# First adaLN part of a diffusion layer: eight channel tiles taken as four pairs, three of them in column blocks, with the context projections summed pair by pair

## Chip, cores and metric

The kernel runs on one core of a Trainium2 chip. The metric is the device time of one execution in microseconds (us). A difference of less than 0.2% (about 2.2 us) cannot be told from no change.

## What is computed

One layer over 1024 latent tokens and 256 context tokens, 1024 channels each. Cut to what the change touches:

```python
sh1, sc1, ... = split(silu(c) @ w_ada + b_ada, 6)            # latents
csh1, csc1, ... = split(silu(c_ctx) @ w_ada + b_ada, 6)      # context
h_l = LN0(x)   * (1 + sc1)  + sh1     # 1024 tokens
h_c = LN0(ctx) * (1 + csc1) + csh1    # 256 tokens
p = h @ W_in                          # context needs only its k, v and gate columns
```

The rest of the layer (gMLP gating, mLSTM, output projection, MLP) follows and is the same in both kernels.

## The kernel before

The first part of the program, about 112 us, makes the shifts and scales `mod1`, the normalized context and its k, v and gate projections, and then the v and gate projection of the eight latent chunks of 128 tokens. After it come the q and k projections of the latents (`qk`).

The reduction over 1024 channels is cut into eight tiles of 128 (`KT` = 8). `ada1_load(j)` (L119) loads, for output channel tile j, the shift and scale columns of `w_ada` for all eight reduction tiles: two loads of 512 KB. `ada1_mm(j)` (L273) multiplies them by the two conditioning vectors, which stand as 2 of 128 columns of a weight tile: five reduction tiles in float32, which TensorE runs as two passes each, and three split into a high and a low part, three products each (`mm3`). The operands are 256 columns wide. `ada1_fin` (L288) transposes the 2x256 result and adds the bias into `mod1`. The eight tiles follow each other on TensorE, and work of the next tile stands between the parts of the last.

Context: `norm_x` normalizes both context tiles on VectorE, with the power on GpSimd; their transposes stand in PSUM until `ctx_affine(j)` (L305) applies `mod1` for each tile, and `ctx_split` (L311) makes the pair `Hhi`, `Hlo` of four tiles at a time. Then come the k projection (`kctx`) and `vg_chunk` (L356) for the two context tiles, each a sum over eight reduction tiles into one PSUM bank, emptied by ScalarE (`kcr`, `va`).

Latents: `lat_h(c)` (L395) normalizes chunk c, transposes it on TensorE (`pt_l`), applies `mod1` in eight ScalarE instructions (`h_l`), casts them to `Hhi` and leaves the rest in `Hlo` on VectorE; `vg_chunk(c)` is then 48 matmuls of 264 columns. A scheduler settles the order on each engine from dependencies and its own estimates; all loads are issued from one queue (SP), in order, and a load waits there for the buffer that it fills.

Of the kernel before, what the change touches and what calls it, by code (L numbers as in the profile page):

```python
# [38 lines left out]
def layer_kernel(ctx: ExitStack, tc: tile.TileContext, I: dict, out: bass.AP, dbg=None):  # L39
    nc = tc.nc  # L40
    V, S, G, T = nc.vector, nc.scalar, nc.gpsimd, nc.tensor

# [45 lines left out]
    def prep_slot(src, n, name, colscale=None):  # L88
        hi = wpool.tile([P, SLOT], F32R, tag="whi", name=f"hi_{name}")
        lo = wpool.tile([P, SLOT], F32R, tag="wlo", name=f"lo_{name}")  # L90
        h = n // 2
        for i in range(2):
            raw = raw_tile(f"raw_{name}_{i}")
            dma(raw[:, :h], src[:, i * h : (i + 1) * h])
            if colscale is not None:
                rv = raw[:, :h].rearrange("p (k c) -> p k c", k=2)
                V.tensor_tensor(rv, rv, colscale.unsqueeze(1).broadcast_to([P, 2, h // 2]), ALU.mult)
            S.copy(hi[:, i * h : (i + 1) * h], raw[:, :h])
            V.tensor_tensor(
                lo[:, i * h : (i + 1) * h], raw[:, :h], hi[:, i * h : (i + 1) * h].bitcast(F32), ALU.subtract  # L100
            )
        return hi, lo
# [8 lines left out]
    def x_tile(name):  # L111
        return sp.tile([P, D], F32, tag="x", bufs=7, name=name)
# [6 lines left out]
    def ada1_load(j):  # L119
        rw = [x_tile(f"wa{j}_{i}") for i in range(2)]  # L120
        for i in range(2):
            dma(rw[i], I["wada1"][j, :, i * D : (i + 1) * D])
        hi = wpool.tile([P, SLOT], F32R, tag="whi", name=f"ahi_{j}").rearrange("p (k c) -> p k c", c=264)
        lo = wpool.tile([P, SLOT], F32R, tag="wlo", name=f"alo_{j}").rearrange("p (k c) -> p k c", c=264)
        rv = [t.rearrange("p (k c) -> p k c", c=256) for t in rw]
        for i in range(2):
            k0 = max(KT - ADA_SPLIT, 4 * i)
            if k0 < 4 * i + 4:
                src, ks = rv[i][:, k0 - 4 * i :, :], slice(k0, 4 * i + 4)
                S.copy(hi[:, ks, 0:256], src)  # L130
                V.tensor_tensor(lo[:, ks, 0:256], src, hi[:, ks, 0:256].bitcast(F32), ALU.subtract)
        ada_w.append((hi, lo, rv))
# [164 lines left out]
    xc = []
    for c in range(NCTX):
        ada1_load(2 + c)
        xc.append(load_x(I["ctx"][c * P : (c + 1) * P, :], f"c{c}"))  # L300
    zc = [norm_x(xc[c], f"c{c}") for c in range(NCTX)]
    zt = None
    hc = [sp.tile([P, KT, P], F32, tag="h32", bufs=2, name=f"hc{c}") for c in range(NCTX)]

    def ctx_affine(j):  # L305
        for c in range(NCTX):
            S.activation(
                hc[c][:, j, :], zt[c][j // 4][:, j % 4, :], AF.Identity, bias=mod1[:, j, 0, 1:2], scale=mod1[:, j, 1, 1:2]
            )

    def ctx_split(k0):  # L311
        for c in range(NCTX):
            sl = slice((ctx_tok + c) * P, (ctx_tok + c + 1) * P)
            S.copy(Hhi[:, k0 : k0 + 4, sl], hc[c][:, k0 : k0 + 4, :])
            V.tensor_tensor(
                Hlo[:, k0 : k0 + 4, sl], hc[c][:, k0 : k0 + 4, :], Hhi[:, k0 : k0 + 4, sl].bitcast(F32), ALU.subtract
            )

    prev = None
    for j in range(KT):  # L320
        if 4 <= j + 3 < KT:
            ada1_load(j + 3)
        if j == 4:
            wK = prep_slot(I["win"][0], 2048, "K")
        ar = ada1_mm(j)
        if j == 3:
            zt = [
                h_transpose(zc[0], [ps_tr("zc0a"), ps_tr("zc0b")]),
                h_transpose(zc[1], [ps_mm(f"zc1{q}").rearrange("p (k t) -> p k t", k=4) for q in range(2)]),
            ]  # L330
        if prev is not None:
            ada1_fin(*prev)
            if prev[0] == 3:
                for q in range(4):
                    ctx_affine(q)
                ctx_split(0)
            if prev[0] > 3:
                ctx_affine(prev[0])
        prev = (j, ar)
# [40 lines left out]


    for b in range(2):
        pm = ps_mm(f"kctx_{b}")
# [4 lines left out]
        S.copy(raw[:, 1:257], pm[:, :256])  # L388
# [3 lines left out]

    xs = [load_x(I["x"][c * P : (c + 1) * P, :], f"l{c}") for c in range(2)]

    def lat_h(c):  # L395
        if c + 2 < NT:
            xs.append(load_x(I["x"][(c + 2) * P : (c + 3) * P, :], f"l{c + 2}"))
        z = norm_x(xs[c], f"l{c}")
        h_tile(sp, z, c, lambda kt: mod1[:, kt, 1, 0:1], lambda kt: mod1[:, kt, 0, 0:1], f"l{c}", 2)

    vg_chunk(ctx_tok, NT)
    lat_h(0)
    vg_chunk(ctx_tok + 1, NT + 1)
    lat_h(1)
# [1277 lines left out]
```

## Time and profile before

| | us |
|---|---|
| median of 3 runs | 1098.2 (1096.82 to 1098.74) |
| the profiled execution | 1095.39 |
| its span, first to last instruction | 1093.4 |
| around the span | 2.0 |
| TensorE busy | 1061.6 (97%) |
| VectorE, ScalarE, GpSimd busy | 744.1, 542.2, 54.9 |

The profiled execution is 2.8 us below the median. Times in the trace count from the start of the span. The mean granted TensorE clock over the span is 0.996 of full speed.

### The profile page before, as it was taken

To read this page: it belongs to the slowest core of one execution; us is meant where nothing else is said; L and a number is where in the kernel's file an instruction comes from. 1 tells how busy PE (TensorE), PEld (TensorE's weight loads), DVE (VectorE), ACT (ScalarE), POOL (GpSimd) and SP (SyncE) were. 2 spreads that over 40 slices of the span, in tenths; PEclk is the share of its full clock that TensorE was granted. 3 is DMA by queue.
4 is the path that set the end of the run, shared out by engine and by line. 5 is a ranking of instruction groups with operands and counts; after the bars stand their busy time and mean duration, and the time that the engine had idled before them with its cause. 6 is when DMAs were issued, how large, how long until landed. Compare 5 with 4: busy or idle time off the path is not lost.

```text
span 1093.4 us, 14625 instructions
## 1 busy us (share of the span) xinstructions
PE 1061.6 (97%) x5279; PEld 882.6 (81%) x5279; DVE 744.1 (68%) x1294; ACT 542.2 (50%) x909; POOL 54.9 (5%) x81
## 2 busy tenths in 40 slices
PE   8999999998989999999999999999999999999996
PEld 6899778777878888878888888888888888888885
DVE  5793576587773477689946556475577556868966
ACT  3576453344451255677756556566444233435511
POOL 0010000001110021100000000000000000001201
PEclk9999999999999999999999999999999999999998
DMA  9783478878683953342726252537996328655501
GB/s 331 253 293 103 125 253 294 265 195 222 150 229 122 315 175 117 106 165 68 269 89 206 93 186 112 173 135 263 361 388 228 116 97 278 207 189 160 207 1 77
DMA packets 92416, 208.09 MB, mean 190 GB/s; under 512 B 10036, under 2 KB 31412, under 8 KB 92088
## 3 DMA queue, kind: packets, MB, share of 16 engines
q1 hardware_dynamic: 92344, 207.16, 57.4%
q8 instruction: 41, 0.67, 0.2%
q14 instruction: 31, 0.25, 0.1%
HBM read 155.91 MB, written 51.21 MB: 189 GB/s over the span
## 4 chain that ended last, share of the span: by engine, by line
PE 84%; DMA 6%; DVE 5%; ACT 3%; POOL 1%; issue 1%; SPq 0%; DVEq 0%; POOLq 0%; ACTq 0%
PE A L1025 30%; PE B L1025 24%; PE wo L218 3%; PE wo L216 3%; PE wo L217 3%; PE pa L279 2%; DMA nmb<-d_rows 2%; PE vg L218 2%; PE vg L217 2%; PE vg L216 2%; PE u L216 1%; DMA ad<-in_wada 1%; PE u L217 1%; PE u L218 1%; DMA raw_V<-in_win 1%; PE n L748 1%
## 5 line engine op out<-in xcount | busy, mean ns | idle before, releaser
L1025 PE MATMUL A<-wh,pb 128*128 128x512 f32 (+1 forms) x528 | 158.9, 383 | 0.0
L1025 PE MATMUL B<-wh,pb 128*128 128x512 f32 x384 | 118.6, 390 | 0.0
L1025 PEld LDWEIGHTS A<-wh,pb 128*128 128x128 f32 x528 | 98.0, 188 | 20.0
L1025 PE MATMUL A<-wl,pb 128*128 128x512 f32 (+1 forms) x264 | 101.4, 384 | 0.4 <-DVE pm L1552 0.4
L1025 PEld LDWEIGHTS B<-wh,pb 128*128 128x128 f32 x384 | 72.1, 188 | 15.6
L1025 PE MATMUL B<-wl,pb 128*128 128x512 f32 x192 | 75.0, 391 | 0.0
L916 POOL TENSOR_TENSOR rs_n<-ve_n,mhalf 128x1 f32<-128x1 f32 x23 | 29.8, 1294 | 708.8 <-DVE ve_n L914 670.2
L1152 DVE TENSOR_TENSOR wc<-w1x,wc 128x512 fp32r<-128x512 f32 x56 | 38.5, 690 | 35.6 <-ACT wc L1151 35.6
L1245 ACT CAST wh<-b 128x1024 fp32r<-128x1024 f32 x40 | 41.8, 1049 | 41.7 <-DVE pb L1246 29.1
L1245 ACT CAST pb<-a_S 128x1024 fp32r<-128x1024 f32 x32 | 33.7, 1052 | 57.9 <-PE B L1025 24.4
L1246 DVE TENSOR_TENSOR wl<-b,wh 128x1024 fp32r<-128x1024 f32 x40 | 48.7, 1222 | 19.3 <-ACT wh L1245 10.2
L1025 PEld LDWEIGHTS A<-wl,pb 128*128 128x128 f32 x264 | 49.6, 188 | 10.9 <-ACT wh L1245 0.8
L216 PE MATMUL wo<-lo_W,yh 128*128 128x512 f32 x128 | 52.1, 407 | 0.0
L1245 ACT CAST pb<-a_A 128x1024 fp32r<-128x1024 f32 x24 | 25.2, 1052 | 54.0 <-PE A L1025 37.4
L218 PE MATMUL wo<-hi_W,yl 128*128 128x512 f32 x128 | 50.6, 395 | 0.0
L217 PE MATMUL wo<-hi_W,yh 128*128 128x512 f32 x128 | 50.5, 394 | 0.0
L1246 DVE TENSOR_TENSOR pb<-a_S,pb 128x1024 fp32r<-128x1024 f32 x32 | 39.1, 1222 | 12.6 <-ACT pb L1245 12.4
L216 PE MATMUL vg<-lo_VG,Hhi 128*128 128x264 f32 x160 | 46.0, 288 | 0.0
L1246 DVE TENSOR_TENSOR pb<-a_A,pb 128x1024 fp32r<-128x1024 f32 x24 | 29.3, 1222 | 24.3 <-ACT pb L1245 24.3
L1151 ACT CAST wc<-w1x 128x512 fp32r<-128x512 f32 x56 | 34.6, 619 | 22.7 <-PE A L1025 11.0
L218 PE MATMUL vg<-hi_VG,Hlo 128*128 128x264 f32 x160 | 45.3, 284 | 0.6 <-DVE Hlo L207 0.6
L217 PE MATMUL vg<-hi_VG,Hhi 128*128 128x264 f32 x160 | 45.4, 284 | 0.0
(417 smaller groups left out, 2705.0 us busy)
## 6 DMA issues: line engine op xcount, KB each, us to landing
ad<-in_wada SPq DMA_DIRECT2D x32, 512.0 KB, 5.4
b<-in_w SPq DMA_DIRECT2D x32, 512.0 KB, 5.0
a_S<-d_S SPq DMA_DIRECT2D x32, 512.0 KB, 4.2
d_S<-hF SPq DMA_DIRECT2D x50, 256.0 KB, 2.3
a_A<-d_A SPq DMA_DIRECT2D x24, 512.0 KB, 5.0
d_A<-hF SPq DMA_DIRECT2D x36, 256.0 KB, 2.1
wa<-in_wada SPq DMA_DIRECT2D x16, 512.0 KB, 7.1
w1y<-in_w SPq DMA_DIRECT2D x16, 512.0 KB, 4.0
```

The costliest lines, as they stand in the source:

```text
L216: T.matmul(o, ahi, blo, start=start, stop=False)
L217: T.matmul(o, ahi, bhi, start=False, stop=False)
L218: T.matmul(o, alo, bhi, start=False, stop=stop)
L279: T.matmul(pa[:, 0:256], s32[:, k, :], rv[k // 4][:, k % 4, :], start=(k == 0), stop=(k == KT - 1))
L748: T.matmul(pn[d][:, hh, :], nmb[:, d, h, :], vc[:, h, :], start=hh == 0, stop=False, skip_group_check=True)
L916: G.tensor_tensor(rs, ve, mhalf[:, :1], op=ALU.pow)
L1025: T.matmul(o, a, b, start=start and i == 0, stop=stop and i == 2, skip_group_check=more)
L1151: S.copy(t[:, 0:512], src)
L1152: V.tensor_tensor(t[:, 512:1024], src, t[:, 0:512].bitcast(F32), ALU.subtract)
L1245: S.copy(hi, src)
L1246: V.tensor_tensor(lo, src, hi.bitcast(F32), ALU.subtract)
```

## The change

The eight channel tiles become four pairs, with 512 columns (two tiles, shift and scale) in each matmul, all in float32. Pair 0 uses the whole array. Pairs 1 to 3 use 32 of its columns for each matmul: reduction tile k stands in column block k mod 4, so four partial sums stand in four blocks of 32 PSUM partitions, and a matmul by `quads` (a 0/1 matrix) adds and transposes them in `ada1_fin`. The split of `w_ada` on ScalarE and VectorE goes away. The context is normalized on ScalarE; transposes, affine step and split go pair by pair (`ctx_tr`, `ctx_h`), and the k, v and gate sums of the context are held open in five PSUM banks and added to as a pair comes (`ctx_k`, `ctx_vg`). The order on TensorE, VectorE and ScalarE is pinned to the order of the code up to the second latent chunk's `Hlo` (`in_order`); what follows on VectorE and ScalarE is queued after it (`queue_after`). The loads of w_ada are four times two of 1 MB.

```diff
-    def ada1_load(j):
...
+    def ada1_load(p):
+        ws = [wpool.tile([P, SLOT], F32, tag=("whi", "wlo")[i], name=f"wa_{p}_{i}") for i in range(2)]
+        for i in range(2):
+            dma(ws[i][:, :2048], I["wada1"][2 * p + i])
+        ada_w.append([w[:, :2048].rearrange("p (k c) -> p k c", c=512) for w in ws])
...
+    def norm_x(xt, name, on_act=False, mvrs=None):
+        mv, rs = mvrs or stats(sp, xt, D, name)
...
+        if on_act:
+            nb = sp.tile([P, 1], F32, tag="nb", name=f"nb_{name}")
+            V.scalar_tensor_tensor(nb, mv[:, 0:1], -1.0, rs, ALU.mult, ALU.mult)
+            S.activation(z, xt, AF.Identity, bias=nb, scale=rs)
...
+    def ada1_mm(p):
+        pa = bank(7, f"pa_{p}")
+        wide = p < ADA_WIDE
         for k in range(KT):
+            rhs = ada_w[p][k // 4][:, k % 4, :]
+            if wide:
+                T.matmul(pa, s32[:, k, :], rhs, start=k == 0, stop=k == KT - 1)
             else:
+                o = 32 * (k % 4)
+                T.matmul(
+                    pa[o : o + 32, :],
+                    s32[:, k, 0:32],
+                    rhs,
+                    start=k < 4,
+                    stop=k >= 4,
+                    tile_position=(0, o),
+                    skip_group_check=True,
                 )
+        n = 2 if wide else P
+        ar = sp.tile([P, 512], F32, tag="arow", name=f"arow_{p}")
+        V.tensor_copy(ar[:n], pa[:n])
         return ar
...
+    pins = ExitStack()
+    pins.enter_context(in_order(T, V, S))
+    ar = ada1_mm(0)
+    zc = [norm_x(xc[c], f"c{c}", True) for c in range(NCTX)]
+    pt = ctx_tr(0)
+    ada1_fin(0, ar)
+    ctx_h(0, pt)
+    pt = ctx_tr(1)
+    ar = ada1_mm(1)
+    wK, wVG = slot_tiles("K"), [slot_tiles("VG0")]
+    slot_half(wK, rawK[0], 2048, 0)
+    ada1_fin(1, ar)
+    slot_half(wK, rawK[1], 2048, 1)
+    rawVG.append(raw_load(I["wvg"][1], 2112, "VG1"))
+    ada1_load(3)
+    xs = [load_x(I["x"][c * P : (c + 1) * P, :], f"l{c}") for c in range(2)]
+    ctx_h(1, pt)
...
+    ctx_k(0)
+    pt = ctx_tr(2)
+    ctx_k(1)
+    ctx_vg(0, 0)
+    ctx_vg(1, 0)
+    ar = ada1_mm(2)
+    ada1_fin(2, ar)
+    ctx_h(2, pt)
+    pt = ctx_tr(3)
...
+    ctx_k(2)
+    ctx_vg(2, 0)
+    ar = ada1_mm(3)
+    ada1_fin(3, ar)
+    mv0 = stats(sp, xs[0], D, "l0")
+    ctx_h(3, pt)
+    for p in range(3):
+        ctx_vg(p, 1)
...
+    zl = [norm_x(xs[0], "l0", False, mv0), norm_x(xs[1], "l1")]
+    lat_h(0, zl[0])
+    ctx_k(3)
+    for i in range(2):
+        ctx_vg(3, i)
...
+    lat_h(1, zl[1])
+    pins.close()
+    queue_after(pins, V, S)
     wQ = prep_slot(I["win"][1], 2048, "Q")
```

Three places show how the built programs stand. The first is TensorE around the normalized context. `pa` is an adaLN sum, `z_c0` and `z_c1` are the two normalized context tiles, `ptc_` their transposes for a pair, `pat` the transposed sum. Before, at the fourth of eight channel tiles:

```order
L279 MATMUL pa_3_330<-wa3_0_211,s32_186 128x256 x4
L279 MATMUL pa_3_330<-wa3_1_212,s32_186 128x256
L197 MATMUL zc0a_347<-cst_95,z_c0_230 128x128 x4
L197 MATMUL zc0b_348<-cst_95,z_c0_230 128x128 x4
L291 MATMUL pat_2_367<-cst_95,arow_2_315 128x2 x2
```

Now, between pair 0 and pair 1:

```order
L307 MATMUL pa_0_209<-wa_0_1_88,s32_181 128x512 x4
L348 MATMUL ptc_0_246<-cst_91,z_c0_229 128x128
L348 MATMUL ptc_0_246<-cst_91,z_c1_242 128x128
...
L328 MATMUL pat_0_251<-cst_91,arow_0_218 128x2 x4
L348 MATMUL ptc_1_263<-cst_91,z_c0_229 128x128
L348 MATMUL ptc_1_263<-cst_91,z_c1_242 128x128
...
L310 MATMUL pa_1_268<-wa_1_0_188,s32_181 32x512 x4
L310 MATMUL pa_1_268<-wa_1_1_189,s32_181 32x512 x4
```

Eight of the sixteen context transposes now stand between the first and the second quarter of the adaLN matmuls; before, the first stood behind half of them.

The second is ScalarE from the cast of latent chunk 0 to the affine step of chunk 1. Before:

```order
L367 COPY va_9_704<-vg_9_0_706 128x2x128
L206 CAST Hhi_107<-h32_l0_693 128x8x128
L367 COPY va_9_704<-vg_9_1_734 128x2x128
L98 CAST hi_Q_797<-raw_Q_0_799 128x1024
L204 ACTIVATE h32_l1_786<-pt_l1_0_776,mod1_109 128x128 x4
```

Now:

```order
L234 CAST Hhi_104<-h32_l0_529 128x8x128
L488 COPY kcr0_576<-kctx_204 128x256
L467 ACTIVATE kct_0_580<-kcr0_576,convw_317 128x256
L470 ACTIVATE kct_0_580<-kct_0_580 128x256
L488 COPY kcr1_586<-kctx_204 128x256
L467 ACTIVATE kct_1_590<-kcr1_586,convw_317 128x256
L470 ACTIVATE kct_1_590<-kct_1_590 128x256
L443 COPY va_8_596<-vgc_0_0_205 128x2x128
L443 COPY va_8_596<-vgc_0_1_207 128x2x128
L443 COPY va_9_605<-vgc_1_0_206 128x2x128
L443 COPY va_9_605<-vgc_1_1_208 128x2x128
L232 ACTIVATE h32_l1_626<-pt_l1_0_616,mod1_106 128x128 x4
```

All ten instructions that empty the context sums (four of them the convolution of k, `kct`) now stand between the two latent chunks. Before, the convolution stood ahead of both chunks, and two `va` copies and one half of the cast of the q weights stood between them.

The third is TensorE at the transposes of latent chunks 2 and 3. Before:

```order
L218 MATMUL vg_0_1_837<-hi_VG1_527,Hlo_108 128x264
L197 MATMUL pt_l2_0_879<-cst_95,z_l2_877 128x128 x4
L197 MATMUL pt_l2_1_880<-cst_95,z_l2_877 128x128 x4
L216 MATMUL vg_1_0_902<-lo_VG0_518,Hhi_107 128x264
```

Now:

```order
L246 MATMUL vg_1_1_770<-hi_VG1_406,Hlo_105 128x264
L225 MATMUL pt_l2_0_719<-cst_91,z_l2_717 128x128 x4
L225 MATMUL pt_l2_1_720<-cst_91,z_l2_717 128x128 x4
L225 MATMUL pt_l3_0_812<-cst_91,z_l3_810 128x128 x4
L225 MATMUL pt_l3_1_813<-cst_91,z_l3_810 128x128 x4
L244 MATMUL vg_2_0_835<-lo_VG0_282,Hhi_104 128x264
```

Before, the transposes of chunk 2 stood one whole chunk of matmuls (`vg_1`) ahead of the matmuls that use them; now they stand behind `vg_1`, and the matmuls of chunk 2 follow at once.

## Rows read from the trace of the kernel before

**Rows 1.** The page: busy time, share of the span and instructions of each engine.

```profile
PE 1061.6 (97%) x5279; PEld 882.6 (81%) x5279; DVE 744.1 (68%) x1294; ACT 542.2 (50%) x909; POOL 54.9 (5%) x81
```

**Rows 2.** Waits of TensorE: total us, times, longest us.

```profile
PE pa L279 <- DMA wa<-in_wada: 4.9, 1, 4.9
PE kctx L216 <- DVE Hlo L315: 1.6, 1, 1.6
```

**Rows 3.** Timeline of TensorE, adaLN and context k: start, us, what.

```profile
4.93 4.40 PE L279 MATMUL pa<-wa,s 128*128 128x256 f32 x10 [4.93 <-DMA wa<-in_wada]
10.23 2.32 PE L279 MATMUL pa<-wa,s 128*128 128x256 f32 x10
...
37.82 0.28 PE L291 MATMUL pat<-cst,arow 2*128 2x2 f32 x2
...
43.38 0.28 PE L217 MATMUL kctx<-Hhi,hi_K 128*128 128x256 f32 x1
43.50 0.28 PE L218 MATMUL kctx<-Hhi,lo_K 128*128 128x256 f32 x1
```

**Rows 4.** Timeline of TensorE, latent chunks to the first qk matmul.

```profile
59.49 0.37 PE L216 MATMUL vg<-lo_VG,Hhi 128*128 128x264 f32 x1
...
61.00 0.39 PE L218 MATMUL vg<-hi_VG,Hlo 128*128 128x264 f32 x1 [0.56 <-DVE Hlo L207]
...
66.42 1.04 PE L197 MATMUL pt_l<-cst,z_l 128*128 128x128 f32 x8
...
73.10 1.04 PE L197 MATMUL pt_l<-cst,z_l 128*128 128x128 f32 x8
...
112.32 0.48 PE L216 MATMUL qk<-Hlo,hi_K 128*128 128x512 f32 x1
```

**Rows 5.** Windows: stretch, length, busy time of engines, granted clock, DMA share, GB/s.

```profile
5.00:15.00 10.00, 10.00 (x46) 8.48 (x47) 3.18 (x7) 2.50 (x3) 0.00 (x0) 1.00 1.01 371
```

**Rows 6.** Timeline of VectorE, single instructions.

```profile
10.43 0.41 DVE L285 COPY arow<-pa 2x256 f32<-2x256 f32 x1 [2.46 <-PE pa L218]
...
20.50 1.28 DVE L187 BATCH_NORM_STATS2 st_c<-x_c 128x6 f32<-128x512 f32 x2
...
23.52 0.81 DVE L259 TENSOR_SCALAR z_c<-x_c,mv_c,rs_c 128x1024 f32<-128x1024 f32 x1 [0.54 <-POOL rs_c L180]
...
38.40 1.20 DVE L99 TENSOR_TENSOR lo_K<-raw_K,hi_K 128x1024 fp32r<-128x1024 f32 x1
...
46.81 0.48 DVE L377 SCALAR_TENSOR_TENSOR kct<-kcr,convw,kct 128x256 f32<-128x256 f32 x1
...
59.73 1.22 DVE L207 TENSOR_TENSOR Hlo<-h_l,Hhi 128x1024 fp32r<-128x1024 f32 x1
...
1073.15 0.68 DVE L1564 TENSOR_TENSOR r<-A,pm 128x512 f32<-128x512 f32 x1
```

**Rows 7.** Timeline of ScalarE, single instructions and groups.

```profile
45.10 0.39 ACT L388 COPY kcr<-kctx 128x256 f32<-128x256 f32 x1
45.52 0.51 ACT L376 ACTIVATE kct<-kcr,convw 128x256 f32<-128x256 f32 x1
...
49.23 0.38 ACT L367 COPY va<-vg 128x256 f32<-128x256 f32 x1 [0.97 <-PE vg L218]
...
67.06 2.91 ACT L204 ACTIVATE h_l<-pt_l,mod 128x128 f32<-128x128 f32 x8
70.00 1.05 ACT L206 CAST Hhi<-h_l 128x1024 fp32r<-128x1024 f32 x1
...
1068.88 1.15 ACT L909 ACTIVATE xt<-r,nmu_n 128x1024 f32<-128x1024 f32 x1 [6.47 <-DVE nmu_n L907]
```

**Rows 8.** End of TensorE's work, and windows after it with the granted clock.

```profile
1083.22 0.40 PE L1025 MATMUL A<-wh,pb 128*128 128x256 f32 x2
...
1084.00:1088.00 4.00, 0.00 (x0) 0.00 (x0) 3.78 (x10) 0.00 (x0) 0.12 (x1) 0.95 0.32 131
1088.00:1092.00 4.00, 0.00 (x0) 0.00 (x0) 2.54 (x4) 0.00 (x0) 0.92 (x1) 0.50 0.32 124
```

More of the change, by code (lines that the diff above doesn't have):

```diff
@@ L1 @@
 import math
-from contextlib import ExitStack
+from contextlib import ExitStack, contextmanager
 import numpy as np
@@ L41, in layer_kernel, with in_order, queue_after @@
     V, S, G, T = nc.vector, nc.scalar, nc.gpsimd, nc.tensor
+    @contextmanager
+    def in_order(*engines):
+        last = nc.cur_bb.bb.instructions[-1]
+        yield
+        traced = nc.cur_bb.bb.instructions
+        first = next(k for k in reversed(range(len(traced))) if traced[k] is last) + 1
+        for e in engines:
+            prev = None
+            for i in traced[first:]:
+                if i.engine == e.engine:
+                    if prev is not None:
+                        tc.add_manual_dep(
+                            i,
+                            prev.name,
+                            mybir.DependencyInfo(mybir.DependencyClass.NoSync, mybir.DependencyReason.DATA),
+                            reason="in_order",
+                        )
+                    prev = i
+    def queue_after(stack, *engines):
+        traced = nc.cur_bb.bb.instructions
+        for e in engines:
+            stack.enter_context(tc.issue_after(next(i for i in reversed(traced) if i.engine == e.engine)))
     def dma(o, i):
@@ L111, in x_tile @@
     def x_tile(name):
[L112 removed]
+        return sp.tile([P, D], F32, tag="x", bufs=6, name=name)
     cc = const.tile([P, KT, 2], F32, name="cc")
@@ L117, in layer_kernel @@
     ada_w = []
-    def ada1_load(j):
-        rw = [x_tile(f"wa{j}_{i}") for i in range(2)]
+    def ada1_load(p):
+        ws = [wpool.tile([P, SLOT], F32, tag=("whi", "wlo")[i], name=f"wa_{p}_{i}") for i in range(2)]
         for i in range(2):
[L122 to L132, printed above, removed]
+            dma(ws[i][:, :2048], I["wada1"][2 * p + i])
+        ada_w.append([w[:, :2048].rearrange("p (k c) -> p k c", c=512) for w in ws])
     ada1_load(0)
-    cst = econ.tile([P, 576], F32, name="cst")
+    cst = econ.tile([P, 578], F32, name="cst")
     dma(cst, I["consts"])
@@ L140, in layer_kernel @@
     onehot = cst[:, 512:576]
+    quads = cst[:, 576:578]
     bada1 = const.tile([P, KT, 2], F32, name="bada1")
     dma(bada1, I["bada1"])
+    V.tensor_scalar(bada1[:, :, 1:2], bada1[:, :, 1:2], 1.0, None, ALU.add)
     mhalf = const.tile([P, NH], F32, name="mhalf")
@@ L277, in ada1_mm @@
+        return z
+    s32 = sp.tile([P, KT, P], F32, tag="s32", bufs=1, name="s32")
+    G.memset(s32, 0.0)
+    V.tensor_copy(s32[:, :, 0:2], sc_s)
+    def ada1_mm(p):
+        pa = bank(7, f"pa_{p}")
+        wide = p < ADA_WIDE
         for k in range(KT):
-            if k < n32:
-                T.matmul(pa[:, 0:256], s32[:, k, :], rv[k // 4][:, k % 4, :], start=(k == 0), stop=(k == KT - 1))
-            else:
-                mm3(
-                    pa[:, 0:256], shi[:, k - n32, :], slo[:, k - n32, :], hi[:, k, 0:256], lo[:, k, 0:256], k == 0, k == KT - 1
-                )
@@ new lines, in ada1_mm, with ada1_fin @@
+        V.tensor_copy(ar[:n], pa[:n])
+        return ar
+    def ada1_fin(p, ar):
+        pt = ps_tr(f"pat_{p}")[:, 0, 0:8]
+        for q in range(4):
+            if p < ADA_WIDE:
+                T.transpose(pt[:, 2 * q : 2 * q + 2], ar[0:2, q * P : (q + 1) * P], ident[0:2, 0:2])
+            else:
+                T.matmul(pt[:, 2 * q : 2 * q + 2], ar[:, q * P : (q + 1) * P], quads, start=True, stop=True)
+        for c in range(2):
+            ks = slice(2 * p, 2 * p + 2)
+            V.tensor_tensor(mod1[:, ks, :, c], pt[:, c::2].rearrange("p (j h) -> p j h", j=2), bada1[:, ks, :], ALU.add)
@@ L295, in layer_kernel @@
     ctx_tok = NT - NCTX
+    xc = [load_x(I["ctx"][c * P : (c + 1) * P, :], f"c{c}") for c in range(NCTX)]
     ada1_load(1)
[L297 to L339, printed above, removed]
+    rawK = raw_load(I["win"][0], 2048, "K")
@@ new lines, in layer_kernel, with ctx_tr, ctx_h @@
+    rawVG = [raw_load(I["wvg"][0], 2112, "VG0")]
+    ada1_load(2)
+    def ctx_tr(p):
+        pt = ps_tr(f"ptc_{p}")
+        for k in range(2):
+            for c in range(NCTX):
+                kt = 2 * p + k
+                T.transpose(pt[:, 2 * k + c, :], zc[c][:, kt * P : (kt + 1) * P], ident)
+        return pt
+    def ctx_h(p, pt):
+        h32 = sp.tile([P, 2, NCTX * P], F32, tag="hc", name=f"hc_{p}")
+        for k in range(2):
+            kt = 2 * p + k
+            src = pt[:, 2 * k : 2 * k + 2, :].rearrange("p a b -> p (a b)")
+            S.activation(h32[:, k, :], src, AF.Identity, bias=mod1[:, kt, 0, 1:2], scale=mod1[:, kt, 1, 1:2])
+        ks, sl = slice(2 * p, 2 * p + 2), slice(ctx_tok * P, NT * P)
+        S.copy(Hhi[:, ks, sl], h32)
+        V.tensor_tensor(Hlo[:, ks, sl], h32, Hhi[:, ks, sl].bitcast(F32), ALU.subtract)
@@ new lines, in hv, with ctx_k @@
+    def hv(x):
+        return x.rearrange("p (k c) -> p k c", k=KT)
+    pkc = bank(0, "kctx").rearrange("p (b t) -> p b t", b=2)
+    pvg = [[bank(b, f"vgc_{c}_{i}") for c, b in enumerate(bs)] for i, bs in enumerate(((1, 2), (5, 6)))]
+    def ctx_k(p):
+        whi, wlo = (hv(x[:, :2048]) for x in wK)
+        sl = slice(ctx_tok * P, NT * P)
+        for kt in (2 * p, 2 * p + 1):
+            for b in range(2):
+                c = slice(b * P, (b + 1) * P)
+                ops = ((whi, Hlo), (whi, Hhi), (wlo, Hhi))
+                for i, (w, h) in enumerate(ops):
+                    T.matmul(
+                        pkc[:, b, :],
+                        w[:, kt, c],
+                        h[:, kt, sl],
+                        start=kt == 0 and b == 0 and i == 0,
+                        stop=kt == KT - 1 and i == 2,
+                        skip_group_check=True,
+                    )
@@ new lines, in ctx_vg @@
+    def ctx_vg(p, i):
+        whi, wlo = (hv(x) for x in wVG[i])
+        for kt in (2 * p, 2 * p + 1):
+            for c in range(NCTX):
+                sl = slice((ctx_tok + c) * P, (ctx_tok + c + 1) * P)
+                mm3(pvg[i][c][:, :264], Hhi[:, kt, sl], Hlo[:, kt, sl], whi[:, kt, :], wlo[:, kt, :], kt == 0, kt == KT - 1)
+    pins = ExitStack()
[3 more added lines that the diff above has]
+    pt = ctx_tr(0)
@@ L391, in layer_kernel @@
         dma(d_k[:, b, D : D + 256], t1)
[L393 to L404, printed above, removed]
+    for c in range(NCTX):
+        va = va_new(NT + c)
+        for i in range(2):
+            vg_ev(NT + c, i, va, pvg[i][c])
+        dma(d_va[NT + c], va)
+    lat_h(1, zl[1])
+    pins.close()
+    queue_after(pins, V, S)
     wQ = prep_slot(I["win"][1], 2048, "Q")
@@ L1593, in _consts @@
 def _consts():
-    c = np.zeros((P, 576), np.float32)
+    c = np.zeros((P, 578), np.float32)
     c[:, 0:128] = np.eye(P, dtype=np.float32)
```

108 lines of the change are left out of this document (50 added, 58 removed).

## The prediction

> **What bounds the kernel now.** The table of engines comes first: TensorE is busy for 97% of the span and VectorE for 68% [rows 1]. So the reader expects that time goes only where TensorE's work shrinks or where TensorE begins to wait. TensorE's list of waits is next: the whole start phase holds two of note, 4.9 us for the first `w_ada` load and 1.6 us for `Hlo` of the context [rows 2]. TensorE's timeline then gives the anchors: the first matmul at 4.93 [rows 3], the first latent chunk's matmuls (`vg_0`) at 59.49 and the first q and k matmul at 112.32 [rows 4]. What follows is the same code in the same order, so I carry a shift there one to one to the end. I work the sum up to the point where the latent chunks run without waits again.
>
> **What the change removes.** A float32 pass of 256 columns took 0.44 us in the first ten (4.40) and 0.23 in the next ten (2.32) [rows 3]. A channel tile of before is ten such passes and nine `mm3` matmuls at about 0.1, near 3.2 us, so eight tiles are 25.8 us of TensorE at its settled pace. Pair 0 is 16 passes of 512 columns, 0.46 each: 7.4 us. For a pair in column blocks no row of this kernel has the duration. The bounds: if no two of its 16 passes overlap, 7.4 us; if all four blocks run abreast, a quarter, 1.86. I take 4.2: a matmul's two passes need the same block and follow each other, but the second may run beside the next matmul's first, which makes nine slots of 0.46. TensorE's own work then shrinks by 25.8 − 7.4 − 3 × 4.2 = 5.8 us.
>
> A rule bears on this choice. The Trainium skill, TensorE: Matmul & The Clock Gate, Part 3, says that matmuls start and end in program order even where tiles run together; with two passes a matmul, that order gives the nine slots. The same skill, TensorEngine Tiling (Array Packing), Theoretical Speedup, allows up to four times for 32 columns, which would be the 1.86. No run here shows either yet.
>
> **What it adds: the waits up to `vg_0`.** All times are on the trace's clock.
>
> - *First load.* The first matmul waited until 0.5 MB had landed [rows 2, 3]. Now it needs 1 MB, 0.52 MB more at 371 GB/s [rows 5]: 1.4 us later, 6.3.
> - *Pair 0.* Five wide passes at the first pace (4.40) and eleven at 0.46: 9.5, to 15.8.
> - *The context behind it.* VectorE's order is pinned, so the copy of pair 0's sum (`arow`) stands ahead of the statistics of both context tiles, although these landed long before. The copy is 2x512: between 0.41 for 2x256 and 0.68 for 128x512, I take 0.6, to 16.4. From the start of a tile's statistics to its `z` took 3.0 us (20.50 to 23.52, with GpSimd's part) [rows 6], and the second tile's stand behind the first's result: 22.5. `z_c1` on ScalarE is 1.15 [rows 7]: 23.7. Then three transposes (0.4, at 1.04 for eight [rows 4]), four small transposes of the sum (0.6, at 0.28 for two [rows 3]), the bias (0.4), two affine steps of 0.51 [rows 7] and the next four transposes (0.5). Pair 1 starts at 26.6, its load hidden: cst, context and pair 1 are 3.4 MB behind pair 0, down by 18.3 at 371 GB/s. TensorE, which worked through this stretch before, is nearly idle from 15.8 to 26.6. This is the largest term.
> - *Pair 1 to pair 2.* Pair 1 ends at 30.8. `arow` 0.68, then `lo_K` 1.20 ahead of the bias on VectorE [rows 6]: the k sums start at 32.7. Twelve matmuls at 0.12 [rows 3], 1.44, and four transposes 0.5: 34.6. `Hlo` of pair 1 is done near 35.3 (bias 0.4, affine 1.0, the cast at half of 1.05 [rows 7], `Hlo` at half of 1.22 [rows 6]), so TensorE waits 0.7; twelve and 24 matmuls, 4.3: pair 2 at 39.7, to 43.9.
> - *Pair 2 to pair 3.* `arow` 0.7, transposes and bias 1.0, affine, cast and `Hlo` 2.2, then 24 matmuls, 2.9: pair 3 at 50.7, to 54.9. Its weights come behind VG1, whose buffers `lo_K` frees at 34.2: 3.2 MB, down by 42.8, hidden.
> - *Pair 3 to `vg_0`.* `arow` and transposes 1.2, 36 matmuls 4.3 (they hide the last `Hlo`), `pt_l0` 1.0, 36 matmuls 4.3, `pt_l1` 1.0: TensorE is ready at 66.8. But `vg_0` writes the PSUM bank of the k sum, which ScalarE empties in its order: `h_l0` from 61.5, 2.91; cast 1.05; `kcr` 0.39; `kct` 0.51 [rows 7]; two steps of the convolution on VectorE, behind `Hlo` (1.22), 0.48 each [rows 6]; `kct` again; the second `kcr`: 68.5. So `vg_0` starts at 68.5, against 59.49 [rows 4]: **+9.0**.
>
> **The waits of the latent chunks.** Before, a chunk took 6.68 us, 66.42 to 73.10, 1.04 for its transposes and 5.64 for 48 matmuls, without a wait but 0.56 in the first [rows 4]. Now `vg_0` ends at 74.2. ScalarE's second chunk stands behind the rest of the convolution (0.51, 0.96 and 0.51) and four `va` copies at 0.38: `h_l1` from 72.0, cast done at 76.0 [rows 7]. TensorE waits **1.8**. `vg_1` ends at 81.6, and now `pt_l2` and `pt_l3` stand directly ahead of `vg_2`: ready at 83.7. `h_l2` starts when `pt_l2` is there and the last `va` copy is done, 82.7; 2.91 and 1.05 later it is 86.7 [rows 7]. That is a wait of **3.0**, 2.5 to 3.9 with the affine steps' start and `z_l3`, for which nothing stood ahead before. Later chunks have the old order. Less the 0.56: 9.0 + 1.8 + 3.0 − 0.6 = 13.2.
>
> **The clock.** After TensorE's last matmul (1083.22 plus 0.40) the granted clock is 0.95 on average to 1088 and 0.50, its lower level, after that [rows 8]. The idle stretch before pair 1 is 10 us with seven transposes in it, so I expect the lower level when pair 1 starts. The first ten passes of the kernel cost 2.1 us more than the next ten [rows 3]; I add 2.1, between 0 (the transposes keep it up) and 4 (the later waits too). The Trainium skill, TensorE: Matmul & The Clock Gate, Part 1, describes the same drop after idling; rows 8 agree with 0.50.
>
> **Sum.** 13.2 + 2.1 = 15.3. The profiled execution took 1095.39 and would take 1110.7; the median of the runs is 2.8 above it, so 1113.5, rounded **1114 us**.
>
> **Rivals.**
>
> - *All four blocks abreast* (1.86 a pair). The pairs lie on the path, so it gives 3 × 2.34 = 7 us back: **1107**. For it: the blocks share nothing but the moving data. Against: every matmul has its own moving data, and two passes. The skill's table named above speaks for it.
> - *Blocks don't overlap*, that is, the change doesn't do what it says. Each pair takes 7.4, 3.2 more: +9.6, **1123**. For it: successive matmuls in the trace follow one another and each streams all 512 columns. The skill's tiling page, Key Properties, adds a drain at every change of mode; a pair changes twice, and no row shows a price.
> - *The other side: TensorE's work decides.* TensorE was busy without a break up to 112 us [rows 1, 4], and 5.8 us of work go, 12.8 with four abreast; if the waits are covered, the time is **1092**, or 1085. It decides if the new waits stay below 5.8 (or 12.8) us in sum. Against it: the stretch from 15.8 to 26.6 alone has 10.8 us with only some 1.5 of matmuls, and its 6.0 us of two statistics in a row are rows, not guesses. If the statistics were ready at once, the stretch would shrink to about 4.
> - *Only the transfers decide* (the later ones, q among them): with a shift of 13 us on TensorE they have that much more time before `qk` at 112.32 [rows 4]; hidden, no price.
>
> **Chances and range.** The forecast, with 1109 to 1118 as its own range, 0.48; four abreast (1104 to 1109) 0.21; no overlap (1118 to 1126) 0.16; the other side 0.08; in between, 1094 to 1104, 0.07. A change of 0.2%, 2.2 us, is about what a measurement tells from none. Faster 0.09, same 0.04, slower 0.87. The range is 1104 to 1124: it takes in the four-abreast case and most of the no-overlap one.
>
> **What would show it.** Pair 1's first matmul near 26 to 27, VectorE's first statistics behind `arow` at about 16.4; the eight 32x512 matmuls of a pair taking 1.9, 4.2 or 7.4 us; the granted clock at 0.50 in a part of 16 to 30; `vg_0` near 68 behind `kcr`; waits of some 2 and 3 us at `vg_1` and `vg_2` for `Hhi`; the first `qk` near 127. I am wrong if pair 1 starts before 22, or if `vg_0` stands before 60.

## The result, and the profile after

| | before | after |
|---|---|---|
| median of 4 runs, us | 1098.03 | 1112.53 (1111.52 to 1115.12) |
| ratio to before, 95% interval | 1 | 1.0137 [1.0117, 1.0156] |
| profiled execution, its span | 1095.39, 1093.4 | 1111.52, 1109.7 |
| TensorE busy | 1061.6 | 1060.4 |
| first matmul of `vg_0`, of `qk` | 59.49, 112.32 | 66.52, 126.77 |

The changed kernel is 1.4% slower; the forecast was 1114. The two profiled executions differ by 16.1 us, and 14.45 of them are there at the first q and k matmul. TensorE's waits up to 130 us, against [rows 2] (total us, times, longest us):

```profile
PE ptc L348 <- ACT z_c L290: 6.7, 2, 4.6
PE pa L307 <- DMA wa<-in_wada: 6.2, 1, 6.2
PE ptc L348 <- ACT hc L356: 2.9, 2, 1.4
PE pat L330 <- DVE arow L321: 2.4, 3, 0.8
PE pt_l L225 <- DVE mv_l L217: 2.0, 1, 2.0
PE vg L244 <- ACT Hhi L234: 1.3, 2, 0.9
PE vg L244 <- ACT kcr L488: 1.3, 1, 1.3
PE kctx L376 <- DVE Hlo L359: 1.0, 2, 0.7
PE vg L246 <- DVE Hlo L235: 0.7, 1, 0.7
```

Before, two totals reached 1 us [rows 2]; here eight do, and the largest is the one for the normalized context. TensorE's timeline says where they lie (start, length):

```profile
6.18 8.84 PE L307 MATMUL pa<-wa,s 128*128 128x512 f32 x16 [6.18 <-DMA wa<-in_wada]
19.59 0.33 PE L348 MATMUL ptc<-cst,z_c 128*128 128x128 f32 x1 [4.57 <-ACT z_c L290]
22.04 0.90 PE L348 MATMUL ptc<-cst,z_c 128*128 128x128 f32 x3 [2.12 <-ACT z_c L290]
22.87 0.58 PE L328 MATMUL pat<-cst,arow 2*128 2x2 f32 x4
24.89 1.12 PE L348 MATMUL ptc<-cst,z_c 128*128 128x128 f32 x4 [1.44 <-ACT hc L356]
25.93 3.64 PE L310 MATMUL pa<-wa,s 128*32 128x512 f32 x16
...
38.90 1.92 PE L310 MATMUL pa<-wa,s 128*32 128x512 f32 x16
...
45.51 0.58 PE L376 MATMUL kctx<-Hlo,hi_K 128*128 128x256 f32 x1 [0.26 <-DVE Hlo L359]
...
50.87 1.92 PE L310 MATMUL pa<-wa,s 128*32 128x512 f32 x16
...
66.52 0.39 PE L244 MATMUL vg<-lo_VG,Hhi 128*128 128x264 f32 x1 [1.28 <-ACT kcr L488]
...
73.52 0.39 PE L244 MATMUL vg<-lo_VG,Hhi 128*128 128x264 f32 x1 [0.93 <-ACT Hhi L234]
...
83.63 1.16 PE L225 MATMUL pt_l<-cst,z_l 128*128 128x128 f32 x8 [2.05 <-DVE mv_l L217]
85.22 0.59 PE L244 MATMUL vg<-lo_VG,Hhi 128*128 128x264 f32 x1 [0.42 <-ACT Hhi L234]
```

The three lines of L310 are the pairs in column blocks: 3.64 us for the first and 1.92 for the others. The windows explain the first, and the 5.36 us from 45.51 to 50.87 for 24 matmuls that take 0.12 each elsewhere (us, length, then busy time of TensorE, its weight loads, VectorE, ScalarE and GpSimd, granted clock, DMA share, GB/s):

```profile
15.00:20.00 5.00, 0.34 (x2) 0.14 (x1) 3.95 (x10) 1.24 (x1) 0.59 (x2) 0.99 1.01 402
20.00:25.00 5.00, 1.52 (x8) 1.11 (x9) 0.39 (x3) 2.39 (x4) 0.52 (x1) 0.50 1.02 429
25.00:30.00 5.00, 4.58 (x20) 1.20 (x20) 1.05 (x2) 2.38 (x3) 0.00 (x0) 0.50 0.25 107
...
40.00:45.00 5.00, 2.75 (x20) 1.68 (x12) 1.16 (x4) 1.91 (x4) 0.00 (x0) 0.88 0.95 367
45.00:50.00 5.00, 4.74 (x23) 4.50 (x22) 2.88 (x3) 1.67 (x2) 0.00 (x0) 0.50 0.88 280
...
80.00:85.00 5.00, 2.75 (x21) 2.10 (x20) 4.85 (x14) 4.16 (x10) 1.74 (x4) 0.98 0.35 136
85.00:90.00 5.00, 4.62 (x20) 4.32 (x21) 5.00 (x7) 4.01 (x10) 0.00 (x0) 0.50 0.44 115
```

The granted clock stood at its lower level three times, each time after TensorE had been partly idle: for most of the 10.9 us between pairs 0 and 1, and for 2.2 of the 5 us from 40 on and from 80 on, before `vg_2`. VectorE shows why the context was late (start, length):

```profile
15.05 0.68 DVE L321 COPY arow<-pa 2x512 f32<-2x512 f32 x1 [5.35 <-PE pa L307]
15.66 1.26 DVE L215 BATCH_NORM_STATS2 st_c<-x_c 128x6 f32<-128x512 f32 x2
...
18.09 0.16 DVE L289 SCALAR_TENSOR_TENSOR nb_c<-mv_c,rs_c 128x1 f32<-128x1 f32 x1 [0.74 <-POOL rs_c L208]
18.17 1.28 DVE L215 BATCH_NORM_STATS2 st_c<-x_c 128x6 f32<-128x512 f32 x2
...
20.55 0.16 DVE L289 SCALAR_TENSOR_TENSOR nb_c<-mv_c,rs_c 128x1 f32<-128x1 f32 x1 [0.67 <-POOL rs_c L208]
```

It waited 5.35 us for pair 0's sum, and only then took the statistics of the context tiles, although both had landed by 11.9 (issued at 3.3 and 3.8, at most 8.1 us to landing).

### The profile page after: what moved, and what is told of

Its sections match the earlier page's. It is cut to its first block, busy times and chain, and to the rows that moved or that the text cites. A ratio compares the mean times of both kernels' runs of the same rounds, so it can differ in the third digit from the quotient of the medians.

```text
span 1109.7 us, 14402 instructions
## 1 busy us (share of the span) xinstructions
PE 1060.4 (96%) x5203; PEld 872.4 (79%) x5203; DVE 734.0 (66%) x1270; ACT 536.4 (48%) x895; POOL 55.4 (5%) x82
## 4 chain that ended last, share of the span: by engine, by line
PE 82%; DMA 5%; DVE 5%; ACT 4%; issue 1%; POOL 1%; SPq 0%; DVEq 0%; ACTq 0%; POOLq 0%
PE A L1121 28%; PE B L1121 24%; PE wo L246 3%; PE wo L244 3%; PE wo L245 3%; PE u L244 1%; PE u L246 1%; PE u L245 1%; PE vg L246 1%; PE vg L245 1%; PE vg L244 1%; DMA nmb<-d_rows 1%; PE n L844 1%; DMA raw_V<-in_win 1%; ACT h_l L232 1%
## 5 line engine op out<-in xcount | busy, mean ns | idle before, releaser
L1342 DVE TENSOR_TENSOR pb<-a_S,pb 128x1024 fp32r<-128x1024 f32 x32 | 39.1, 1222 | 13.9 <-ACT pb L1341 13.7
L1121 PEld LDWEIGHTS B<-wl,pb 128*128 128x128 f32 x192 | 36.0, 188 | 7.7
L244 PE MATMUL vg<-lo_VG,Hhi 128*128 128x264 f32 x128 | 38.2, 298 | 2.6 <-ACT Hhi L234 1.3
L509 DVE SCALAR_TENSOR_TENSOR adacc<-ad,silu_cc,adacc 128x1024 f32<-128x1024 f32 x28 | 35.7, 1276 | 6.3 <-DMA ad<-in_wada 6.1
## 6 DMA issues: line engine op xcount, KB each, us to landing
wa<-in_wada SPq DMA_DIRECT2D x8, 1024.0 KB, 13.9
```

Source lines behind the costliest of these rows:

```text
L244: T.matmul(o, ahi, blo, start=start, stop=False)
L509: V.scalar_tensor_tensor(adacc, wt, sc_s[:, kt, 0:1], adacc, ALU.mult, ALU.add)
L1121: T.matmul(o, a, b, start=start and i == 0, stop=stop and i == 2, skip_group_check=more)
L1342: V.tensor_tensor(lo, src, hi.bitcast(F32), ALU.subtract)
```

## The experiments

But for the last three, each has one edit, or one group of edits, to the changed kernel. Times of `vg_0` and `qk` are the starts of their first matmuls in the profiled execution, against 66.52 and 126.77. All ratios are to the kernel before, run on the same chip; the changed kernel's is 1.0137.

**The column blocks.** Theory: the pairs lie on the path, and what they cost is how far the blocks overlap. Three runs: no blocks; the two reduction tiles of a block directly behind each other; all eight in one block (its sum is then copied and transposed as pair 0's, which the cut below leaves out).

```diff
-ADA_WIDE = 1
+ADA_WIDE = 4
```

> All four pairs use the whole array; the column blocks are gone, the rest stays. Theory (the blocks run four abreast and lie on the path): a pair takes 7.4 us at the full clock instead of 1.9, so three pairs cost 12 to 16 us more, less up to 4 us because TensorE's longer work keeps the clock up: first q and k matmul at 136 to 143, time 1121 to 1129. Rival (other engines hide the adaLN matmuls): under 4 us more.

```diff
-        for k in range(KT):
+        for k in (0, 4, 1, 5, 2, 6, 3, 7):
```

> In pairs 1 to 3 the two reduction tiles that share a column block follow each other directly (0, 4, 1, 5, 2, 6, 3, 7). Theory (matmuls start in order, and the same block must be free): a pair takes five times 0.92, 4.6 us, instead of 1.9 at the full clock; the time rises by 6 to 10 us, to 1119 to 1122. Rival (the array takes ready matmuls of other blocks ahead): a pair stays at 1.9 and the time at 1112.5.

```diff
-                o = 32 * (k % 4)
-                T.matmul(pa[o : o + 32, :], s32[:, k, 0:32], rhs, start=k < 4, stop=k >= 4, ...)
+                T.matmul(pa[0:32, :], s32[:, k, 0:32], rhs, start=k == 0, stop=k == KT - 1, tile_position=(0, 0))
```

> Pairs 1 to 3 keep weights of 32 columns, but all eight reduction tiles stand in column block 0 and add into the same 32 partitions; the sum is then transposed as for pair 0. Theory (four different blocks work at the same time): with one block a pair is serial again, 16 passes of 0.46, 7.4 us at the full clock instead of 1.9, and the time 1121 to 1129, as with the whole array. Rival (32 columns of weights are quicker by themselves, wherever they stand): a pair stays near 1.9 and the time at 1112.

Without blocks: 1126.34, ratio 1.0271 [1.0252, 1.0290], `qk` at 140.8. In one block: 1124.77, 1.0264 [1.0248, 1.0279], `qk` at 140.7. In the other order: 1113.28, 1.0149 [1.0126, 1.0173], `qk` at 127.6, the same as the changed kernel. The pairs 2 and 3 in TensorE's timeline, with the whole array, with one block, and in the other order:

```profile
45.35 7.03 PE L307 MATMUL pa<-wa,s 128*128 128x512 f32 x16
...
61.74 7.41 PE L307 MATMUL pa<-wa,s 128*128 128x512 f32 x16
```

```profile
45.35 7.05 PE L309 MATMUL pa<-wa,s 128*32 128x512 f32 x16
...
61.90 7.20 PE L309 MATMUL pa<-wa,s 128*32 128x512 f32 x16
```

```profile
39.86 1.94 PE L310 MATMUL pa<-wa,s 128*32 128x512 f32 x16
...
51.77 1.94 PE L310 MATMUL pa<-wa,s 128*32 128x512 f32 x16
```

So 32 columns of weights save nothing by themselves (7.05); four blocks at once save nearly three quarters (1.92), in either order of the tiles: my expectation of 4.6 for the other order fell. The blocks are worth 14 us at `qk`. They are not what makes the change slow; they hide how slow the rest of it is.

**The statistics on VectorE.**

```diff
-    ar = ada1_mm(0)
     zc = [norm_x(xc[c], f"c{c}", True) for c in range(NCTX)]
+    ar = ada1_mm(0)
```

> The statistics of both context tiles stand ahead of pair 0's sum on VectorE; nothing else changes. Theory (the order on VectorE makes the idle stretch before pair 1): the statistics start when the tiles land, about 11, z_c1 is ready near 17 instead of 22, pair 1 starts at 20 to 21 instead of 25.9, and the first q and k matmul at 119 to 122 instead of 126.8; the time is 1105 to 1108, against 1112.5 of the changed kernel. Rival (the idle stretch is hidden by a later wait: weights of the next pairs, or ScalarE's emptying of the sums): pair 1 starts earlier, but the q and k projection within 1 us of 126.8.

1103.26, ratio 1.0057 [1.0037, 1.0077], below the 1105 to 1108 expected: two lines in the other order win 0.8 of the 1.37% lost, some 9 us. `vg_0` at 60.33, `qk` at 120.5, pair 1 at 20.05, so the trace has 6.3 us of the 9 at `qk`; where the rest lies isn't shown. Its VectorE:

```profile
10.76 1.28 DVE L215 BATCH_NORM_STATS2 st_c<-x_c 128x6 f32<-128x512 f32 x2 [0.97 <-DMA x_c<-in_ctx]
...
15.67 0.16 DVE L289 SCALAR_TENSOR_TENSOR nb_c<-mv_c,rs_c 128x1 f32<-128x1 f32 x1 [0.67 <-POOL rs_c L208]
15.74 0.67 DVE L321 COPY arow<-pa 2x512 f32<-2x512 f32 x1
```

The statistics now lie under pair 0, and its sum is copied only 0.7 us later than before the edit. The rival (a later wait takes it back) is out.

**The clock alone.** Matmuls that nobody reads fill TensorE's idle time and move nothing else, first between pairs 0 and 1, then behind pair 2 too.

```diff
+    warm(4)
     pt = ctx_tr(0)            # and two before its second transpose
     ada1_fin(0, ar)
     ctx_h(0, pt)
+    warm(1)
     pt = ctx_tr(1)
```

> Seven float32 matmuls of 512 columns on data that nobody reads fill TensorE's idle time between pair 0 and pair 1 (four before the first context transpose, two before the second, one before the transposes for pair 1). No operation is left out. Theory (the lower clock level after idling is a cost of its own): the granted clock stays near 1.00 from 15 to 35, pair 1 takes 1.9 instead of 3.6 us, and the first q and k matmul comes 2 to 4 us earlier, 123 to 125; the later drops at 45 and 85 stay. Rival (the waits alone make the loss): the same start of pair 1 and no change beyond 1 us.

```diff
     ar = ada1_mm(2)
+    warm5(1, 448)
     ada1_fin(2, ar)
     ctx_h(2, pt)
+    warm5(1, 512)
+    warm5(1, 256)
     pt = ctx_tr(3)
```

> As the run with the idle time before pair 1 filled, and three more float32 matmuls that nobody reads (448, 512 and 256 columns) in the waits behind pair 2, 0.8 and 1.4 us. No operation is left out and none is moved. Theory (the lower clock after each idle stretch is a cost of its own): the granted clock stays near 1.00 from 15 to 60, the 24 matmuls of the k and v/gate sums before pair 3 take 2.9 us instead of 5.4, vg_0 starts 2 to 3 us earlier than with the first stretch alone (63.8), at 61 to 62, and the first q and k matmul at 120.5 to 122. Rival (the second drop has another cause than the idle time): the clock falls at 43 to 45 as before, vg_0 at 63 to 64.

The first: 1108.98, 1.0116 [1.0086, 1.0145], an interval that overlaps the changed kernel's, so its time alone proves nothing; its trace has `vg_0` at 63.79 and `qk` at 123.85, 2.9 earlier. With both stretches filled: 1104.36, 1.0069 [1.0046, 1.0091], clear of the changed kernel's. `vg_0` is at 62.79, outside the 61 to 62 expected, since pair 0 happened to end at 16.27, 1.25 later than in the changed kernel; from there to `vg_0` it is 46.5 us, against 51.5. Windows of the run with both filled, and pairs 1 and 3 of it:

```profile
20.00:25.00 5.00, 3.76 (x14) 1.67 (x14) 1.45 (x7) 2.49 (x4) 0.56 (x1) 1.00 1.03 427
25.00:30.00 5.00, 3.81 (x30) 1.91 (x30) 2.51 (x3) 3.07 (x5) 0.00 (x0) 1.00 0.28 116
...
45.00:50.00 5.00, 4.18 (x37) 2.54 (x35) 2.38 (x3) 0.21 (x1) 0.00 (x0) 1.00 0.99 368
```

```profile
26.19 1.92 PE L310 MATMUL pa<-wa,s 128*32 128x512 f32 x16
...
44.04 0.39 PE L378 MATMUL kctx<-Hlo,hi_K 128*128 128x256 f32 x1 [0.72 <-DVE Hlo L361]
...
47.12 1.92 PE L310 MATMUL pa<-wa,s 128*32 128x512 f32 x16
```

The clock stays at 1.00, pair 1 takes 1.92, and the 24 matmuls before pair 3 take 3.1 us instead of 5.36. The lower clock up to `vg_0` is 5.0 us of the loss: 1.7 at pair 1, 1.0 in the stretch before it and 2.3 before pair 3. The waits for other engines behind the pairs are still there.

**The waits behind the pairs, and the latents.** Useful work in place of idle time: pairs 2 and 3 ahead of the v and gate sums.

```diff
+    ar = ada1_mm(2)
     ctx_vg(0, 0)
-    ctx_vg(1, 0)
-    ar = ada1_mm(2)
     ada1_fin(2, ar)
+    ctx_vg(1, 0)
     ctx_h(2, pt)
...
+    ar = ada1_mm(3)
     ctx_vg(2, 0)
-    ar = ada1_mm(3)
```

> Pairs 2 and 3 start ahead of the context's v and gate sums that stood before them (24 and 12 matmuls), which now lie in the time in which their own results are copied, transposed and applied. Theory (TensorE's waits behind each pair, 0.81 and 1.44 us, and the lower clock from 45 to 50 can be covered by work that is there): the k sum of pair 2 starts 2.5 to 3 us earlier, the clock stays up, the first q and k matmul at 121 to 123.5. Rival (weights for pairs 2 and 3 arrive too late to start earlier): pair 2 waits for its load, and the gain is under 1 us.

1105.69, 1.0104 [1.0074, 1.0135]; `vg_0` at 61.41, `qk` at 121.2, as the theory had it. Its four runs spread from 1102 to 1110, so the time's interval still touches the changed kernel's.

Next, again on the changed kernel alone, the statistics of latent chunk 2 early and the cast and split of q late, together (the line that passes `zl[2]` on is left out):

```diff
+    zl.append(norm_x(xs[2], "l2"))
     lat_h(1, zl[1])
     pins.close()
     queue_after(pins, V, S)
-    wQ = prep_slot(I["win"][1], 2048, "Q")      # now behind lat_h(3)
```

> The statistics and normalization of latent chunk 2 stand in VectorE's idle time ahead of Hlo of chunk 1, and the cast and split of the q weights go behind chunk 3's affine step. Theory (chunk 3's transposes waited 2.05 us because VectorE came late, and the clock fell after it): the transposes of chunk 2 stand ahead of vg_1 again, the waits before vg_2 go, the granted clock stays near 1.00 from 80 to 95, and the first q and k matmul comes 5 to 7 us earlier, 120 to 122. Rival (ScalarE's chain of affine steps binds): under 2 us.

1108.28, 1.0103 [1.0071, 1.0136], an interval that still touches the changed kernel's; the trace tells more. In this execution the first low clock lasted until 38.7, so `vg_0` was late (68.88); from `vg_0` to `qk` it took 53.2 us, against 60.25 in the changed kernel and 52.8 before. The latents' loss is gone but for 0.4: chunk 2's transposes stand ahead of `vg_1` again (75.51), and `vg_2` starts without a wait. Which of the two moves does it, this run doesn't show.

And the late half of what empties the context sums (the convolution, the second copies of `va`) behind `lat_h(1)` (the edit in words):

```diff
-    (convolution of k, va of both halves)
+    (kcr copies, va of the first half)
     lat_h(1, zl[1])
+    (convolution of k, va of the second half)
```

> On ScalarE and VectorE the two copies of the context k sum and the first half of the context's v and gate sums stay ahead of latent chunk 1; the convolution of k and the second half go behind it. Theory (chunk 1's affine step stands behind the emptying of the context sums): vg_0 starts 1.0 to 1.5 us earlier (near 65.2), vg_1 loses its waits of 0.93 and 0.7, and the first q and k matmul is at 123.5 to 125, unless what is won is lost again at chunk 2, whose statistics are still behind the cast of q. Rival (chunk 2 is what binds): vg_0 and vg_1 earlier, but vg_2 still near 85 and the q and k projection within 1 us of 126.8.

1113.03, 1.0159 [1.0135, 1.0183], `qk` at 127.0: nothing. From pair 3 to `vg_0` it took 14.2 us instead of 15.65, as the theory had it, and `vg_1` began without its waits, but its second half, 24 matmuls later, got a new one:

```profile
79.54 0.56 PE L244 MATMUL vg<-lo_VG,Hhi 128*128 128x264 f32 x1 [3.94 <-DVE gf L446]
```

The rival's number held (`qk` within 1 us), but not for its reason: it is chunk 1 that waits here. VectorE came to the gate columns of chunk 0, which free the PSUM bank, only behind the split of q (`lo_Q`, 76.91 to 79.25). The clock, too, was back later in this execution (last section).

**Together.** The four edits that move work (the statistics, pairs 2 and 3, the latents, the emptying) and a fifth that was not run alone, pair 1 ahead of its context transposes; the same without the emptying; and all five with two filling matmuls:

```diff
+    ar = ada1_mm(1)
     pt = ctx_tr(1)
-    ar = ada1_mm(1)
```

> Together: the statistics of the context ahead of pair 0's sum, pair 1 ahead of its context transposes, pairs 2 and 3 ahead of the v and gate sums, the late half of the emptying behind latent chunk 1, chunk 2's statistics early and the cast of q late. Theory (the places are apart from each other, so their gains add: 6.3 at the statistics, 5 at the pairs, 7 at the latents, 1 to 2 for the rest, read from the first q and k matmul): the first q and k matmul at 104 to 109, ahead of the 112.3 of before, and the time 1088 to 1095. Rival (the gains overlap, since they win back the same lower clock, and the loads of later weights come too late for earlier pairs): the first q and k matmul at 110 to 115, and no difference from the kernel before that can be told.

> As the combination, but the emptying of the context sums and the convolution stand ahead of latent chunk 1, as in the changed kernel. Theory (once chunk 2 no longer binds, ScalarE's order does): 1 to 3 us slower than the combination, from the waits for kcr and for Hhi at vg_0 and vg_1. Rival (the emptying only moves a wait): within 1 us of it.

> As the combination, with two float32 matmuls of 512 columns on data that nobody reads between the first and the second context transpose. Theory (what is left of the idle time before pair 1 still lowers the clock): pair 1 takes 1.9 us, the time is 1 to 3 us below the combination. Rival (the shorter idle time leaves the clock at its upper level): the same within 0.5 us.

| | median us | before, same chip | ratio | `qk` at |
|---|---|---|---|---|
| all | 1090.17 | 1097.52 | 0.9946 [0.9925, 0.9968] | 107.3 |
| without the late emptying | 1092.34 | 1097.52 | 0.9951 [0.9934, 0.9969] | 106.6 |
| all, with filling | 1091.58 | 1097.52 | 0.9951 [0.9936, 0.9967] | 107.3 |

All three beat both kernels: the ratio falls from 1.0137 to 0.9946, some 21 us against the changed kernel, and half a per cent against the one before. The combination is inside what was expected of it. Between the variants the times decide nothing: the medians of the two variants lie 1.4 and 2.2 us above the combination's, their ratios only 0.0005 (0.5 us), and each interval is about 2 us to either side. So the 1 to 3 us expected of the emptying are neither shown nor refuted, and the filling shows no gain; pair 1 of the combination starts at 17.96 and takes 1.92 without it:

```profile
17.96 1.92 PE L310 MATMUL pa<-wa,s 128*32 128x512 f32 x16
...
63.60 0.40 PE L244 MATMUL vg<-lo_VG,Hhi 128*128 128x264 f32 x1 [2.88 <-ACT va L443]
```

The second line is a wait of 2.9 us that is left, in the second half of `vg_1`, at a PSUM bank that is emptied late (in the run with filling the same wait is 2.8 and ends with VectorE's `gf`). The run without the late emptying doesn't have it, but has three smaller ones instead, 2.2 us in sum (`kcr` 1.29, `z_l` 0.57, `Hlo` 0.32), and its `qk` is 0.75 earlier.

## Why the forecast held, and where two of its terms were wrong

| step | forecast | measured |
|---|---|---|
| first matmul; pair 0 ends | 6.3; 15.8 | 6.18; 15.02 |
| `z_c1` ready; pair 1 | 23.7; 26.6 | 22.0; 25.93 |
| pair 2; pair 3 | 39.7; 50.7 | 38.90; 50.87 |
| `vg_0` (+9.0) | 68.5 | 66.52 (+7.0) |
| waits at `vg_1`, `vg_2` | 1.8, 3.0 | 0.93 + 0.7, 2.05 + 0.42 |
| a pair | 4.2 | 1.92, at the lower clock 3.64 |
| lower clock, whole loss | 2.1 | about 7.5 |
| `qk` | +15.3 | +14.45 |

- **The idle stretch before pair 1**, the largest term, was right in place and cause: 10.8 forecast, 10.9 measured, and with the statistics first 4.8 are left, where the prediction had about 4. That the size fits so well is partly luck. A tile's statistics took 2.4 us, not 3.0 [rows 6]: in the 3.0 of before VectorE waited for another tile's sum and copied it between the two ends (first line below). Transposes at the lower clock took about as much more (2.6 against 1.5).
- **The pair was mis-sized.** Nine slots, 4.2 us, was wrong; the rival with four abreast was right: 1.92 for pairs 2 and 3, and for pair 1 where the clock was up. That alone is 3 × 2.3 = 6.8 us too much in the sum. The Trainium skill, TensorEngine Tiling (Array Packing), Theoretical Speedup, has up to four times; the runs show 7.05 / 1.92 = 3.7. My nine slots leaned on a rule of the Trainium skill, TensorE: Matmul & The Clock Gate, Part 3, that matmuls start and end in program order. The rule doesn't give them, since four abreast can start and end in order too. And the run with the other order goes against it: there a matmul of a busy block stood ahead of those of free blocks and did not hold them up (1.94, not 4.6).
- **The clock was mis-sized the other way.** I took one drop, at the first pace of the kernel; there were three. Pair 1 cost 1.7 more (3.64 less 1.92), the small transposes around it 1.0 (2.60 in three rows, against 1.62 with the idle time filled), the 24 matmuls before pair 3 2.3 (5.36 less the 3.08 with the stretch filled), and `vg_2` about 2.5 (from 85.22 to 94.57 with three transposes in it, some 8.3 us of matmuls that take 5.8 at 0.12 each; an estimate, no run changes this alone). In sum 7.5. The two errors, −6.8 and +5.4, nearly cancel: that 15.3 came so near to 14.45 is luck. With both put right it would be 13.9; the other terms make up the 0.5 that is left.
- **The queue behind the sums** was right: `vg_0` waited for `kcr` (1.28), `vg_1` for `Hhi`. So was chunk 2: its transposes stood behind `vg_1`, ScalarE's affine step could begin only with them, and its cast ended at 85.17, just before `vg_2` (last two lines). The longer wait of TensorE there, 2.05 for VectorE's statistics of chunk 3, lies under this one: without it `vg_2` would still have waited for `Hhi`. What the prediction doesn't have is VectorE behind the split of q: `z_l` of chunk 2 was ready only at 80.43, so its transposes couldn't have come ahead of `vg_1`. The run with these statistics early and q late brought them there.
- **The rival on the other side** decided where I said, at the sum of the new waits: with most of the waits taken away the same blocks are 0.54% faster than the kernel before, 5.9 us, or 1092 on the scale of the forecast. With four abreast the rival was priced at 12.8 us, 1085; less than half of that is reached.

```profile
22.38 0.41 DVE L285 COPY arow<-pa 2x256 f32<-2x256 f32 x1 [0.36 <-PE pa L218]
```

```profile
81.19 2.90 ACT L232 ACTIVATE h_l<-pt_l,mod 128x128 f32<-128x128 f32 x8 [0.17 <-PE pt_l L225]
84.12 1.05 ACT L234 CAST Hhi<-h_l 128x1024 fp32r<-128x1024 f32 x1
```

The first line is VectorE before, the other two are ScalarE of the changed kernel.

The wait for loads never showed: pairs 2 and 3 could start earlier without a wait for weights. The shift was not carried one to one to the end: behind `qk` the first `kv` matmul waited 2.2 us for VectorE's `kw`, 0.7 before. What stays open: from the first `kv` to the first `wo` matmul the profiled executions differ by up to 7.6 us (211.7 to 219.3) in code that nothing here changes, so a gain at `qk` does not always stand whole in a single time.

## What to carry to other kernels

Read the order on every engine, not only on the one that is to be relieved: a pinned order put two statistics of 2.4 us behind a sum that they didn't need, and that alone cost 6 us at `qk`, some 9 in the time, of a change whose blocks save 14. When TensorE's work shrinks, put what it has left into the gaps, since each idle stretch here cost its own length and then a slower clock on what followed. And price each term from both sides: a sum can be right while its terms are not, and only the terms say what to mend.

## What the runs showed of the hardware

Four float32 matmuls of 32 columns in four column blocks run abreast, two passes each, in either order of the tiles: eight of them with 512 columns took 1.92 or 1.94 us, against 7.05 in one block. Changing from the whole array to the blocks cost little: pair 2 started 0.21 us after the start of the last matmul before it (38.69 to 38.90), where matmuls of that kind follow each other at 0.12. The way back lies under a wait for `arow` and isn't shown.

How long the lower clock stayed differed between executions of the same instructions: in the changed kernel it was 0.98 again from 30 to 35, in the run with the emptying late, whose program is the same up to there, it was lower until 37.7, with TensorE busy but for 0.8 us from 26 on:

```profile
30.00:35.00 5.00, 4.19 (x23) 4.12 (x20) 3.37 (x6) 1.85 (x4) 0.00 (x0) 0.50 0.34 107
35.00:40.00 5.00, 5.00 (x34) 5.00 (x34) 2.94 (x3) 1.74 (x2) 0.00 (x0) 0.73 0.94 353
```

That run's pair 2 was 2.35 us later (41.25), and only 0.5 of it was there at pair 1 (26.43); the rest, nearly 2 us, is as much as many an edit is worth; the granted clock belongs beside every comparison of two profiles.
